# An expert stage with its SBUF divided anew: six buffers instead of three for split weight pieces, 22 weight slabs in turn instead of 26

## The chip, the cores and the metric

The kernel runs on one core of a Trainium2 chip. Its engines are TensorE (PE in the profile; PEld is its weight load), VectorE (DVE), ScalarE (ACT), GpSimd (POOL) and SyncE (SP). Each has a queue of its own that runs strictly in order, and waits for the others through semaphores. The metric is the device time of one execution in microseconds (us); the time of a kernel is the median of several executions.

## What is computed

One block of a model: a token mixer (retention and an mLSTM, 512 tokens and 16 meta tokens, width 1024), then a layer of 16 experts in which each expert chooses its 66 tokens, then a norm. The change lies in the expert layer:

```python
def _rmsnorm(x, g):
    xf = x.astype(jnp.float32)
    y = xf * lax.rsqrt(jnp.mean(xf * xf, axis=-1, keepdims=True) + EPS)
    return (y * g.astype(jnp.float32)).astype(x.dtype)

def _expert_choice_ffn(h, norm_g, w_router, w_gate, w_up, w_down):
    b_, n_, _ = h.shape
    u = _rmsnorm(h, norm_g)
    aff = jax.nn.softmax(jnp.einsum('bnd,de->bne', u, w_router).astype(jnp.float32), axis=-1)
    cap = EC_CAPACITY * n_ // N_EXPERTS
    g, idx = lax.top_k(jnp.swapaxes(aff, 1, 2), cap)
    xs = jax.vmap(lambda ub, ib: ub[ib])(u, idx)
    hid = (jax.nn.silu(jnp.einsum('becd,edf->becf', xs, w_gate))
           * jnp.einsum('becd,edf->becf', xs, w_up))
    y = jnp.einsum('becf,efd->becd', hid, w_down) * g[..., None].astype(h.dtype)
    return jnp.zeros_like(h).at[jnp.arange(b_)[:, None, None], idx].add(y)

def reference(x, meta_tokens, ...):
...
    h = jnp.concatenate([meta, x], axis=1)
    for l in range(DEPTH):
        h = h + _token_mixer(h, mix_norm_g[l], w_in[l], ...)
        h = h + _expert_choice_ffn(h, ffn_norm_g[l], w_router[l], w_gate[l], w_up[l], w_down[l])
    h = _rmsnorm(h, final_norm_g)
    return h[:, N_META:]
```

Here n_ is 528, cap is 66, and an expert's hidden width is 2816. All of it is float32.

## The kernel before

**Stages.** The mixer and the routing take the first 437 us or so. The rest is the expert stage, `experts` (L852 ff.), with its SBUF laid out by `expert_memory` (L733 to L749).

**An expert.** Its weights (34.6 MB) come through SBUF as 48 slabs of 128 x 1408 float32 (704 KB each): eight for the first half of w_gate, eight for the first half of w_up, eight and eight for the second halves, sixteen for w_down. `weights` (L873) takes the next slab space in turn and issues the load on SP's queue (L878; three of them on POOL, L877). The spaces in turn are `ring`, 26 slabs, after a first pass over 29 spaces (`order`, L748); a load must wait until VectorE, the last reader of a space, is done with it.

**Pieces.** The products are made exact to float32 by splitting both operands into a rounded high part and a remainder. `product` (L892) cuts each slab into two or three pieces (768 and 640 columns; 512, 512 and 384 at the first slab of eight; w_down's cuts rotate). For each piece `split` (L885) has ScalarE copy it to h (L888) and VectorE subtract h from the slab into l (L889); then TensorE multiplies the 66 tokens' high part with h (L903), their low part with h (L904), and their high part with l (L905). The buffers for h and for l are a ring of three each, in the space `pieces` (L860 and L861, `right5t` in the profile). A piece can thus be split only when the piece three before it has been multiplied.

**Order within an expert.** In `experts`, for expert e: w_gate's first half, silu on ScalarE (`gate`, L937); w_up's first half, product on VectorE (`up`, L943); two slabs of w_gate's second half, then `hidden(hT, 0)`, which transposes hid on TensorE (L949), copies it on ScalarE (L952) and takes the remainder on VectorE (L953); the rest of w_gate and w_up; three slabs of w_down, then `hidden(hT, 1)` and `gather(e + 1)`, whose eight transposes (L916) are followed by VectorE's gains (L921) and ScalarE's copies (L922); the rest of w_down; `scatter`, in which ScalarE scales the two output halves (L1006) and POOL adds them to the rows in DRAM. The stretch around the transposes of `hidden(hT, 1)` and `gather` is called the boundary below.

**The last expert** goes through w_down twice, for one half of the output columns each (`last_down`). `combine(0)` adds the first half to the rows between: ScalarE scales (L992), TensorE multiplies by a selection (L998, L999), VectorE adds (L1000), ScalarE squares (L1059).

**What sets the order.** The program's text gives the dependences; a scheduler with a simulated clock then orders each engine's instructions, so that buffers added in one place can move instructions in another. The names in the profile: `left25t` is hid, `left26t` to `left29t` are `low`, `left30t` holds the tokens' high and low parts, `left31t` the output rows, `left32t` to `left53t` the slabs of `mid`, `left54t` and `left55t` the two of `early`, `left56t` the transposed hid.

Of the kernel before, what the change touches and what calls it, by code (L numbers as in the profile page):

```python
# [9 lines left out]
F32R = mybir.dt.float32r  # L10
# [28 lines left out]
PIECE = 768  # L39
# [693 lines left out]
def expert_memory(left, ctx):  # L733
    P = 128

    def slabs(stack, n):
        return [left.open(stack, SLAB).tile(P, SLAB) for _ in range(n)]

    brief = ExitStack()
    hid, = slabs(ctx, 1)  # L740
    low = slabs(ctx, 4)
    xs = left.open(ctx, 2 * KT * CAP, F32R)
    y_rows = left.open(ctx, 2 * D).t
    mid = slabs(ctx, 22)
    early = slabs(brief, 2)
    up = mid[::-1]
    ring = up[:12] + low + up[12:]
    order = itertools.chain(ring[:7], [hid], ring[7:16], early, ring[16:], itertools.cycle(ring))  # L748
    return brief, hid, xs, (order, len(ring)), [t[:, :D] for t in mid[7:0:-1]], mid[0], y_rows  # L749


# [100 lines left out]
def experts(tc, a, bcast, left, right, routed, u_rows, h_rows, out):  # L852
    nc = tc.nc
    P = 128
# [3 lines left out]
    with ExitStack() as ctx:  # L858
        ps = ctx.enter_context(tc.tile_pool(name="eps", bufs=1, space=PSUM, reuse_waits="tile"))
        pieces = right.open(ctx, 6 * PIECE, F32R)  # L860
        p_h, p_l = pieces.ring(3, P, PIECE), pieces.ring(3, P, PIECE)  # L861
        x_h, x_l = xs.tile(P, KT, CAP), xs.tile(P, KT, CAP)
        xf = xf.rearrange("p (k c) -> p k c", c=CAP)
        g_exp = moe.tile(P, KT)
# [15 lines left out]

        def bank(tag="wide"):
            return ps.tile([P, 512], F32, name=tag, bufs=6 if tag == "wide" else 2)

        def split(src):
            n = src.shape[1]  # L885
            h = next(p_h)[:, :n]
            l = next(p_l)[:, :n]
            nc.scalar.activation(h, src, AF.Copy)  # L888
            nc.vector.tensor_sub(l, src, h)  # L889
            return h, l  # L890
# [34 lines left out]
        def wide(w, e, half):  # L925
            src = w[e].rearrange("(p k) f -> p k f", k=KT)
            banks = [bank() for _ in range(3)]
            for k in range(KT):
                slab = weights(src[:, k, half * SLAB:(half + 1) * SLAB])
                product(slab, 0, (512, 1024) if k == 0 else (768,),  # L930
                        lambda c: (banks[c], x_h[:, k], x_l[:, k], k == 0, k == KT - 1))
                yield banks

        def gate(banks):
            for c, b in enumerate(banks):
                n = min(512, SLAB - 512 * c)
                nc.scalar.activation(hid[:CAP, 512 * c:512 * c + n], b[:CAP, :n], AF.Silu)  # L937

        def up(banks):
            for c, b in enumerate(banks):  # L940
                n = min(512, SLAB - 512 * c)
                s = slice(512 * c, 512 * c + n)
                nc.vector.tensor_mul(hid[:CAP, s], b[:CAP, :n], hid[:CAP, s])  # L943

        def hidden(hT, half):
            for f0, fn in ((0, 6), (6, 5)):
                b = bank("wide" if half else "narrow")
                for j in range(fn):
                    nc.tensor.transpose(b[:, j * CAP:(j + 1) * CAP], hid[:CAP, f0 + j:SLAB:RH], ident[:CAP, :CAP])  # L949
                v = b[:, :fn * CAP].rearrange("p (k c) -> p k c", c=CAP)  # L950
                s = slice(RH * half + f0, RH * half + f0 + fn)
                nc.scalar.activation(hT[:, 0, s], v, AF.Copy)  # L952
                nc.vector.tensor_sub(hT[:, 1, s], v, hT[:, 0, s])  # L953
# [49 lines left out]
        def scatter(e, banks):  # L1003
            y = next(y_rows)
            for i, b in enumerate(banks):
                nc.scalar.activation(y[:, 512 * i:512 * i + 512], b[:CAP], AF.Copy, scale=val_t[:CAP, e:e + 1])  # L1006
            nc.gpsimd.indirect_dma_start(  # L1007
                out=h_rows, out_offset=bass.IndirectOffsetOnAxis(ap=idx_t[:CAP, e:e + 1], axis=0),
                in_=y, in_offset=None, compute_op=ALU.add)

        def run(steps, n=None):
            out = None
            for out in itertools.islice(steps, n):
                pass
            return out
# [4 lines left out]
        for e in range(E):  # L1020
            g = wide(a["w_gate"], e, 0)
            gate(run(g))
            up(run(wide(a["w_up"], e, 0)))
            g = wide(a["w_gate"], e, 1)
            run(g, 2)
            if hT is None:
                brief.close()
                space = left.open(ctx, 2 * FT * CAP, F32R).t
                hT = space.rearrange("p (a b c) -> p a b c", b=FT, c=CAP)
            hidden(hT, 0)  # L1030
            gate(run(g))
            up(run(wide(a["w_up"], e, 1)))
            if e == E - 1:
                break
            d = down(e, hT)
            run(d, 3)
            hidden(hT, 1)
            gather(e + 1)
            scatter(e, run(d))
# [8 lines left out]
        slabs = itertools.cycle([next(slabs) for _ in range(n_slabs - 5)])  # L1048
# [98 lines left out]
```

## Time and profile before

| | |
|---|---|
| median of 3 runs | 2024.74 us (2024.28 to 2026.84) |
| the profiled execution's own time | 2024.38 us |
| its span in the trace | 2022.7 us |
| busy: PE, PEld, DVE, ACT, POOL | 96%, 74%, 89%, 75%, 17% |
| DMA, the weight queue q1 | 76.1% of 16 engines' span |
| chain that ended last, by engine | PE 73%, DVE 2%, ACT 2%, issue 1% |

Busy shares are averages over the whole span. The chain is followed back from the last instruction, at each step to what released it. A matmul's row gives the time until its modelled end, which overlaps with the next one's start.

### The profile page before, as it was taken

Reading aid. Unit: us, or ns where it says so; the run is one execution under the profiler, and the core shown is the slowest. Engines: PE = TensorE matmul, PEld = TensorE weight load, DVE = VectorE, ACT = ScalarE, POOL = GpSimd, SP = SyncE. Lnnn points to the kernel's source line nnn. Section 1 sums busy time; section 2 is a strip of 40 time slices with the busy share of each in tenths; the row PEclk is TensorE's granted clock in tenths of the full one; section 3 lists DMA queues with packets and bytes.
Section 4 is the critical chain, followed back from the end, with each engine's and each line's share of the span. In section 5 each row is a group of like instructions: output and inputs, shape, how many; then the busy total and the mean of one; then the engine's idle time right before and its main releaser. Section 6 shows DMA issues by size and latency. Waiting matters only on the chain.

```text
span 2022.7 us, 34626 instructions
## 1 busy us (share of the span) xinstructions
PE 1935.0 (96%) x11841; PEld 1494.8 (74%) x11841; DVE 1793.8 (89%) x2612; ACT 1515.4 (75%) x2398; POOL 335.5 (17%) x301
## 2 busy tenths in 40 slices
PE   7888899959999999999999999999999999999997
PEld 7888899847777777777777767676777776767674
DVE  8999988469999999999999898989898989898988
ACT  4455445358888888888888888888888888888886
POOL 4677764400000000000000000000000000000002
PEclk9999999979999999999999999999999999999998
DMA  4222224698999999999999999999999999999971
GB/s 147 81 64 80 75 75 145 252 345 313 359 365 374 354 381 352 383 351 375 360 366 361 360 358 362 356 364 346 366 343 366 347 365 351 365 352 361 345 254 69
DMA packets 136772, 606.25 MB, mean 300 GB/s; under 512 B 19887, under 2 KB 20527, under 8 KB 136595
## 3 DMA queue, kind: packets, MB, share of 16 engines
q1 hardware_dynamic: 125827, 570.55, 76.1%
q10 hardware_dynamic: 6656, 22.29, 3.2%
q0 software_dynamic: 4112, 11.21, 2.4%
q8 instruction: 92, 1.51, 0.3%
q14 instruction: 85, 0.70, 0.1%
HBM read 593.41 MB, written 10.57 MB: 299 GB/s over the span
## 4 chain that ended last, share of the span: by engine, by line
PE 73%; DVE 2%; ACT 2%; issue 1%; POOL 0%; POOLq 0%; DVEq 0%; ACTq 0%
PE wide L903 16%; PE wide L904 15%; PE wide L905 15%; PE narrow L905 8%; PE narrow L903 8%; PE narrow L904 8%; ACT right5t L888 2%; DVE right5t L889 1%; PE wide L949 1%; PE narrow L949 1%; PE wide L916 1%; DVE left25t L943 0%; DVE left56t L953 0%; ACT wide L1059 0%; POOL right3t L1065 0%
## 5 line engine op out<-in xcount | busy, mean ns | idle before, releaser
L904 PE MATMUL wide<-right5t,left30t 128*66 128x256 f32 (+2 forms) x1984 | 639.2, 327 | 0.0
L903 PE MATMUL wide<-right5t,left30t 128*66 128x256 f32 (+2 forms) x1984 | 624.1, 329 | 5.9 <-ACT right5t L888 1.7
L905 PE MATMUL wide<-right5t,left30t 128*66 128x256 f32 (+2 forms) x1984 | 497.3, 328 | 0.1
L903 PEld LDWEIGHTS wide<-right5t,left30t 128*66 128x66 f32 x1984 | 270.8, 137 | 102.7 <-ACT right5t L888 24.5
L905 PEld LDWEIGHTS wide<-right5t,left30t 128*66 128x66 f32 x1984 | 265.9, 137 | 92.2 <-DVE right5t L889 2.8
L903 PE MATMUL narrow<-right5t,left56t 128*66 128x512 f32 x884 | 307.6, 352 | 2.7 <-ACT right5t L888 2.7
L904 PEld LDWEIGHTS wide<-right5t,left30t 128*66 128x66 f32 x1984 | 270.3, 136 | 52.6 <-issue 0.4
L904 PE MATMUL narrow<-right5t,left56t 128*66 128x512 f32 x884 | 302.4, 352 | 0.0
L905 PE MATMUL narrow<-right5t,left56t 128*66 128x512 f32 x884 | 268.8, 354 | 3.6 <-DVE right5t L889 3.2
L909 POOL DMA_INDIRECT right3t<-u_rows,right3t x16 | 15.7, 981 | 939.0 <-PE narrow L905 457.6
L903 PEld LDWEIGHTS narrow<-right5t,left56t 128*66 128x66 f32 x884 | 122.5, 139 | 58.7 <-ACT right5t L888 3.5
L904 PEld LDWEIGHTS narrow<-right5t,left56t 128*66 128x66 f32 x884 | 122.7, 139 | 55.8 <-issue 3.1
L905 PEld LDWEIGHTS narrow<-right5t,left56t 128*66 128x66 f32 x884 | 114.0, 141 | 57.6 <-DVE right5t L889 12.7
L210 PE MATMUL pj<-right1t,left2t 128*128 128x256 f32 (+1 forms) x512 | 149.3, 292 | 0.6 <-DVE left24t L382 0.6
L212 PE MATMUL pj<-right1t,left3t 128*128 128x272 f32 (+1 forms) x512 | 149.5, 292 | 0.1
L211 PE MATMUL pj<-right2t,left2t 128*128 128x272 f32 (+1 forms) x512 | 148.8, 291 | 0.0
L369 POOL TENSOR_TENSOR left3t<-left1t,left2t 128x1024 fp32r<-128x1024 f32 x38 | 98.4, 2590 | 57.5 <-ACT left2t L368 49.1
L210 PEld LDWEIGHTS pj<-right1t,left2t 128*128 128x128 f32 x512 | 99.5, 195 | 0.8 <-DVE left24t L382 0.7
L212 PEld LDWEIGHTS pj<-right1t,left3t 128*128 128x128 f32 x512 | 99.0, 193 | 0.5 <-DVE left3t L369 0.4
L211 PEld LDWEIGHTS pj<-right2t,left2t 128*128 128x128 f32 x512 | 99.2, 194 | 0.1
L1007 POOL DMA_INDIRECT h_rows<-left31t,right3t x15 | 22.4, 1496 | 415.3 <-ACT left31t L1006 415.3
L943 DVE TENSOR_TENSOR left25t<-wide,left25t 66x512 f32<-66x512 f32 (+1 forms) x96 | 58.5, 637 | 19.2 <-PE wide L905 19.2
(405 smaller groups left out, 4294.9 us busy)
## 6 DMA issues: line engine op xcount, KB each, us to landing
left1t<-in_w_in_f ACTq DMA_DIRECT2D x30, 512.0 KB
left29t<-in_w_gate SPq DMA_DIRECT2D x11, 704.0 KB
left41t<-in_w_gate SPq DMA_DIRECT2D x11, 704.0 KB
left38t<-in_w_gate SPq DMA_DIRECT2D x11, 704.0 KB
left37t<-in_w_gate SPq DMA_DIRECT2D x11, 704.0 KB
left52t<-in_w_up SPq DMA_DIRECT2D x11, 704.0 KB
left51t<-in_w_up SPq DMA_DIRECT2D x11, 704.0 KB
left53t<-in_w_gate SPq DMA_DIRECT2D x10, 704.0 KB
```

The costliest lines, as they stand in the source:

```text
L210: nc.tensor.matmul(ps[:, :ln], wh, x_h[:, k, l0:l0 + ln], start=(k == 0), stop=False)
L211: nc.tensor.matmul(ps[:, :ln], wh, x_l[:, k, l0:l0 + ln], start=False, stop=False)
L212: nc.tensor.matmul(ps[:, :ln], wl, x_h[:, k, l0:l0 + ln], start=False, stop=(k == KT - 1))
L369: eng.tensor_sub(l, t, h)
L888: nc.scalar.activation(h, src, AF.Copy)
L889: nc.vector.tensor_sub(l, src, h)
L903: nc.tensor.matmul(o, xh, h[:, w], start=start, stop=False)
L904: nc.tensor.matmul(o, xl, h[:, w], start=False, stop=False)
L905: nc.tensor.matmul(o, xh, l[:, w], start=False, stop=last)
L943: nc.vector.tensor_mul(hid[:CAP, s], b[:CAP, :n], hid[:CAP, s])
L949: nc.tensor.transpose(b[:, j * CAP:(j + 1) * CAP], hid[:CAP, f0 + j:SLAB:RH], ident[:CAP, :CAP])
L1007: nc.gpsimd.indirect_dma_start(out=h_rows, out_offset=bass.IndirectOffsetOnAxis(ap=idx_t[:CAP, e:e + 1], axis=0), in_=y, in_offset=None, c ...
```

## The change

`expert_memory` makes 18 slabs of `mid` instead of 22 and six of `early` instead of two. The six are used first, once each; the spaces in turn are 22 instead of 26. The first pass has 29 spaces as before. In expert 0, when `brief` (the early slabs' space) is closed, `more_pieces` opens a second piece space there, `left57t`, with three more buffers for h and three more for l; from then on the ring of each is six: three on the right, three on the left. `left56t` stays the transposed hid; the early slabs are now `left50t` to `left55t`. From L885 on, line numbers are 6 higher than before, from L1040 on 7.

```diff
@@ -741,11 +741,11 @@
     low = slabs(ctx, 4)
     xs = left.open(ctx, 2 * KT * CAP, F32R)
     y_rows = left.open(ctx, 2 * D).t
-    mid = slabs(ctx, 22)
-    early = slabs(brief, 2)
+    mid = slabs(ctx, 18)
+    early = slabs(brief, 6)
     up = mid[::-1]
-    ring = up[:12] + low + up[12:]
-    order = itertools.chain(ring[:7], [hid], ring[7:16], early, ring[16:], itertools.cycle(ring))
+    ring = up[:8] + low + up[8:]
+    order = itertools.chain(early[::-1], ring[:1], [hid], ring[1:], itertools.cycle(ring))
     return brief, hid, xs, (order, len(ring)), [t[:, :D] for t in mid[7:0:-1]], mid[0], y_rows
 
 
@@ -858,7 +858,8 @@
     with ExitStack() as ctx:
         ps = ctx.enter_context(tc.tile_pool(name="eps", bufs=1, space=PSUM, reuse_waits="tile"))
         pieces = right.open(ctx, 6 * PIECE, F32R)
-        p_h, p_l = pieces.ring(3, P, PIECE), pieces.ring(3, P, PIECE)
+        halves = [[pieces.tile(P, PIECE) for _ in range(3)] for _ in range(2)]
+        p_h, p_l = map(itertools.cycle, halves)
         x_h, x_l = xs.tile(P, KT, CAP), xs.tile(P, KT, CAP)
         xf = xf.rearrange("p (k c) -> p k c", c=CAP)
         g_exp = moe.tile(P, KT)
@@ -880,6 +881,11 @@
 
         def bank(tag="wide"):
             return ps.tile([P, 512], F32, name=tag, bufs=6 if tag == "wide" else 2)
+
+        def more_pieces():
+            nonlocal p_h, p_l
+            a = left.open(ctx, 6 * PIECE, F32R)
+            p_h, p_l = (itertools.cycle(v + [a.tile(P, PIECE) for _ in range(3)]) for v in halves)
 
         def split(src):
             n = src.shape[1]
@@ -1027,6 +1033,7 @@
                 brief.close()
                 space = left.open(ctx, 2 * FT * CAP, F32R).t
                 hT = space.rearrange("p (a b c) -> p a b c", b=FT, c=CAP)
+                more_pieces()
             hidden(hT, 0)
             gate(run(g))
             up(run(wide(a["w_up"], e, 1)))
```

VectorE in expert 12, from the up-products of the second half (before L943, then L949) over the boundary (gains L921, then L927; remainders of hid L953, then L959); the pieces' remainders are L889, then L895. Before:

```order
L943 TENSOR_TENSOR left25t<-wide,left25t 66x512
L943 TENSOR_TENSOR left25t<-wide,left25t 66x384
L889 TENSOR_TENSOR right5t<-left46t,right5t 128x512
L889 TENSOR_TENSOR right5t<-left46t,right5t 128x384
L889 TENSOR_TENSOR right5t<-left45t,right5t 128x640
L921 TENSOR_TENSOR right3t<-wide,right3t 128x264
L953 TENSOR_TENSOR left56t<-wide,left56t 128x396
L921 TENSOR_TENSOR right3t<-wide,right3t 128x264
L889 TENSOR_TENSOR right5t<-left45t,right5t 128x768
L953 TENSOR_TENSOR left56t<-wide,left56t 128x330
L889 TENSOR_TENSOR right5t<-left44t,right5t 128x768
```

and with the change:

```order
L949 TENSOR_TENSOR left25t<-wide,left25t 66x512
L949 TENSOR_TENSOR left25t<-wide,left25t 66x384
L895 TENSOR_TENSOR right5t<-left42t,right5t 128x512
L895 TENSOR_TENSOR right5t<-left42t,right5t 128x384
L895 TENSOR_TENSOR right5t<-left26t,right5t 128x640
L895 TENSOR_TENSOR left57t<-left26t,left57t 128x768
L927 TENSOR_TENSOR right3t<-wide,right3t 128x264
L959 TENSOR_TENSOR left56t<-wide,left56t 128x396
L927 TENSOR_TENSOR right3t<-wide,right3t 128x264
L959 TENSOR_TENSOR left56t<-wide,left56t 128x330
L895 TENSOR_TENSOR left57t<-left27t,left57t 128x768
```

The fifth remainder of w_down (768 columns) now stands ahead of the gains; before, it stood behind these and the first remainder of hid.

ScalarE in the last expert, at the silus of the first half (before L937, then L943); the pieces' copies are L888, then L894. Before:

```order
L888 ACTIVATE right5t<-left35t 128x640
L888 ACTIVATE right5t<-left34t 128x512 x2
L937 ACTIVATE left25t<-wide 66x512
L888 ACTIVATE right5t<-left34t 128x384
L937 ACTIVATE left25t<-wide 66x512
L937 ACTIVATE left25t<-wide 66x384
L888 ACTIVATE right5t<-left33t 128x768
```

and with the change:

```order
L894 ACTIVATE right5t<-left37t 128x640
L894 ACTIVATE right5t<-left36t 128x512
L894 ACTIVATE left57t<-left36t 128x512
L894 ACTIVATE left57t<-left36t 128x384
L943 ACTIVATE left25t<-wide 66x512 x2
L943 ACTIVATE left25t<-wide 66x384
L894 ACTIVATE left57t<-left35t 128x768
```

The copy of the third piece of w_up's first slab (384 columns) stood between the first silu and the second; it now stands ahead of the three.

ScalarE in expert 0, at the fourth to seventh slab of w_gate's first half, with the change:

```order
L894 ACTIVATE right5t<-left52t 128x768
L894 ACTIVATE right5t<-left52t 128x640
L894 ACTIVATE right5t<-left51t 128x768
L894 ACTIVATE left57t<-left41t 128x640
L894 ACTIVATE right5t<-left51t 128x640
L894 ACTIVATE left57t<-left40t 128x768
L894 ACTIVATE left57t<-left40t 128x640
L894 ACTIVATE right5t<-left50t 128x768
L894 ACTIVATE right5t<-left50t 128x640
L894 ACTIVATE right5t<-left49t 128x768
L894 ACTIVATE right5t<-left49t 128x640
```

Three copies into the new buffers, of the last slab of the first pass's `up[8]` and its neighbour (`left41t`, `left40t`), stand among those of `left51t` and `left50t`; in the program's text they belong to w_gate's second half, fourteen slabs later. Before, the copies of expert 0 followed the order of the slabs. VectorE's remainders move in the same way.

## Rows read from the trace of the kernel before

**Rows 1.** The page, busy time, share of the span and instructions of each engine.
```profile
PE 1935.0 (96%) x11841; PEld 1494.8 (74%) x11841; DVE 1793.8 (89%) x2612; ACT 1515.4 (75%) x2398; POOL 335.5 (17%) x301
```

**Rows 2.** The chain of waits: start us, us on the chain, what.
```profile
503.63 0.23 PE narrow L903
...
506.66 0.88 PE wide L916 x8
...
1083.77 0.88 PE wide L916 x8
...
1378.70 0.88 PE wide L916 x8
...
1873.84 0.88 PE wide L916 x8
```

**Rows 3.** Busy by stretch: length, PE, PEld, DVE, ACT, POOL, PEclk, DMA share, GB/s.
```profile
506.50:602.70 96.20, 95.95 (x573) 71.43 (x572) 89.02 (x121) 81.30 (x123) 4.56 (x4) 1.00 0.98 366
1083.60:1181.90 98.30, 97.15 (x572) 71.04 (x572) 88.30 (x121) 81.31 (x124) 4.99 (x4) 1.00 0.97 358
1379.00:1478.00 99.00, 98.16 (x572) 72.01 (x572) 88.47 (x120) 81.48 (x123) 4.53 (x4) 0.98 0.97 356
```

**Rows 4.** Weight queue: its waits (500 to 1900; us, times, longest), one slab's issue, first use.
```profile
SPq L878 <- DVE right5t L889: 1117.5, 685, 3.9
...
1339.18 0.33 SPq L878 DMA_DIRECT2D left52t<-in_w_down  x1
...
1393.43 1.15 ACT L888 ACTIVATE right5t<-left52t 128x512 fp32r<-128x512 f32 x2
```

**Rows 5.** Waits of the stretch 1181.9 to 1280.2: us in total, times, longest.
```profile
PEld wide L903 <- ACT right5t L888: 2.2, 4, 0.6
...
PEld narrow L905 <- DVE right5t L889: 1.2, 3, 0.6
...
PEld wide L949 <- DVE left25t L943: 0.6, 1, 0.6
```

**Rows 6.** Timeline behind the scatter: start, us, what, [idle before, releaser].
```profile
1212.86 1.24 ACT L1006 ACTIVATE left31t<-narrow,right3t 66x512 f32<-66x512 f32 x2
...
1214.19 0.57 PE L905 MATMUL wide<-right5t,left30t 128*66 128x512 f32 x2
1214.89 0.45 PE L903 MATMUL wide<-right5t,left30t 128*66 128x512 f32 x1
```

**Rows 7.** Timeline at the silus of the first half.
```profile
1229.69 1.47 ACT L888 ACTIVATE right5t<-left53t 128x768 fp32r<-128x768 f32 x2
...
1230.11 0.34 PE L905 MATMUL wide<-right5t,left30t 128*66 128x384 f32 x1
1230.59 0.45 PE L903 MATMUL wide<-right5t,left30t 128*66 128x512 f32 x1
```

**Rows 8.** Timeline at the first up-product.
```profile
1245.03 0.85 ACT L888 ACTIVATE right5t<-left45t 128x768 fp32r<-128x768 f32 x1 [0.49 <-DVE right5t L889]
...
1245.92 0.45 PE L903 MATMUL wide<-right5t,left30t 128*66 128x512 f32 x1 [0.17 <-ACT right5t L888]
```

**Rows 9.** Timeline at the boundary.
```profile
1278.82 1.55 PE L949 MATMUL wide<-right3t,left25t 66*128 66x66 f32 x11 [0.27 <-DVE left25t L943]
...
1279.75 0.81 DVE L889 TENSOR_TENSOR right5t<-left33t,right5t 128x640 fp32r<-128x640 f32 x1
```

**Rows 10.** Busy by stretch, just behind the boundary of expert 10.
```profile
1379.66:1383.10 3.44, 3.44 (x13) 2.32 (x12) 3.44 (x7) 2.60 (x6) 2.75 (x3) 0.51 0.82 264
```

**Rows 11.** Timeline of the last expert, combine(0).
```profile
1990.87 0.60 ACT L1059 ACTIVATE wide<-left35t 128x512 f32<-128x512 f32 x1 [1.96 <-DVE left35t L1000]
...
1993.34 1.13 ACT L888 ACTIVATE right5t<-left28t 128x512 fp32r<-128x512 f32 x2
...
1994.00 0.62 PE L903 MATMUL narrow<-right5t,left56t 128*66 128x512 f32 x1 [2.26 <-ACT right5t L888]
...
1995.55 0.69 PE L905 MATMUL narrow<-right5t,left56t 128*66 128x512 f32 x1 [0.50 <-DVE right5t L889]
...
2000.14 0.45 PE L905 MATMUL narrow<-right5t,left56t 128*66 128x512 f32 x1 [0.69 <-DVE right5t L889]
```

## The prediction

> **What bounds the kernel now.** I read the page first: TensorE is busy for 96% of the span [rows 1], so what can be won is idle TensorE time and time at a low clock. Second, the chain of waits, for the period of an expert. The eight transposes of the next expert's tokens start at 506.66, 1083.77, 1378.70 and 1873.84 us [rows 2]; six experts lie between the first two, three between the next two, five between the last two. Counted from one such start to the next, experts 1 to 6 take (1083.77 - 506.66)/6 = 96.19 us each, experts 7 to 9 take 98.31, experts 10 to 14 take 99.03. The work is the same in each; 2.1 and 2.8 us per expert are waiting or a low clock. Third, busy time by stretch: in an early expert VectorE works 89.02 of 96.20 us and the DMA engines are busy 0.98 of the time, in a late one 88.30 of 98.30 and 0.97 [rows 3]. VectorE has 7 to 10 us to spare per expert, so it is not the bound over an expert, only after bursts. Fourth, the weight queue: from 500 to 1900 us it waited 685 times for VectorE to free a slab, and no row has an engine waiting for a weight transfer; one slab issued at 1339.18 was first read at 1393.43, 54 us later [rows 4].
>
> Fifth, what TensorE waits for in a late expert. The waits of the stretch 1181.9 to 1280.2 give its weight loads four waits for ScalarE's copy of a piece (h), three for VectorE's remainder (l), and one for VectorE's up-product before the hidden transposes [rows 5]. I call them by place:
> - **B**, after the scatter's scaling. ScalarE scales both output halves from 1212.86 (1.24 us) and only then copies the next piece. A 512-column matmul takes 0.23 us of the chain [rows 2], a 384-column one 0.17 by its columns; so TensorE would be done with the pair begun at 1214.19 (512 and 384 columns) at about 1214.60, and goes on at 1214.89: 0.29 us [rows 6].
> - **C** and **E**, after each half's silu. ScalarE comes to the next piece only at 1229.69, behind its silus; TensorE could go on 0.17 after 1230.11 and does at 1230.59: 0.30 us [rows 7]. E is the same 33 us later.
> - **D**, the first up-product. The copy of the next piece waits 0.49 us for VectorE to free a buffer, starts at 1245.03 and holds TensorE until 1245.92: 0.33 us [rows 8].
> - **A**, the three waits for l just after the boundary: the burst of seven VectorE operations there (three up-products, two gains, two remainders of hid) puts l late, 1.2 us at the weight loads [rows 5]; I put two thirds of it, 0.8, on the matmuls, as a weight load runs ahead of its matmul.
> - **F**, the boundary itself: the transposes of hid wait for the third up-product, 0.27 us on the row of the transposes [rows 9], 0.6 at their weight load [rows 5]; I take 0.45.
> Together 2.5 us, which with the jitter of the rest is the 2.1 us above the early experts. In experts 10 to 14 the clock is granted at half (0.51, 1.2 instead of 2.4 GHz) for 3.44 us just behind F [rows 10]; that would cost 3.44 x 0.49 = 1.7, but wait A hides behind it, so that the period grows by 0.72 only.
>
> **The change part by part.**
> Four slabs fewer in turn. A slab is then asked for 22 slabs ahead of its use instead of 26. A slab lasts 96.2/48 = 2.0 us, so the 54 us between issue and use shrink by 4 x 2.0 = 8 to about 46 [rows 4]. The queue's wait for VectorE stays the last one: cost 0. If this cover were gone, each missing slab would cost its 2 us; I price that at nothing since 46 us remain, and a loss would need transfers several times later than now.
>
> Early slabs in expert 0. Six instead of two slabs are used once; they come first, so their space is free when the piece buffers are opened in it. The first pass is 29 slabs either way. Cost 0.
>
> Three pieces pulled forward in expert 0. The order shows pieces of left41t and left40t split between those of left51t and left50t, some fourteen slabs before they are needed. They put 3 pieces on VectorE (0.81 for 640 columns [rows 9], so 2.5 us) and on ScalarE ahead of pieces TensorE needs at once, while only three buffers serve these. TensorE loses 0 (if the lead of two pieces of 0.7 covers it, and the gain of three finished pieces later is used) to 2.5 us. I take +1.2, near the middle, since two pieces' lead is 1.4 us and 2.5 - 1.4 = 1.1.
>
> Six buffers in experts 1 to 3: the order keeps copies and remainders some six pieces ahead. Today's early experts lose little, so 0.
>
> Experts 4 to 6: the order of the late experts begins here at expert 5, not at 7, expert 4 changing over. They leave 96.2 for the new late period, worked out next: 96.7, +0.5 each, +1.5.
>
> Experts 7 to 9: what goes? C and E: the third piece of the next slab was copied between the silus, now all three are copied ahead of them; ScalarE then does the second and third silu as soon as their bank is complete, some 0.3 us earlier, and copies the next piece in time: 0.30 each goes. D goes (0.33), as the copy no longer waits for a buffer. A: VectorE now does one more piece ahead of the burst, 0.8 us, so about 0.6 of the 0.8 goes. B stays: ScalarE's two scalings begin as soon as the last matmul of the output ends, and the copy of the fourth piece follows them in the new order as in the old. F stays: TensorE's order there is unchanged, and VectorE's up-products wait for TensorE's own last bank. So 0.60 + 0.33 + 0.6 = 1.5 to 1.6 of 98.31 goes, to 96.7: 3 x -1.6 = -4.8. Bounds: none goes (0), or the period becomes that of the best rows, 96.19 (-6.4).
>
> The Trainium skill, Perfetto Trace Analysis, section Optimization Strategy, says that the same gap repeating on the engine that should be saturated can mean there is not enough SBUF for the next tile (the number of buffers). By it all six gaps would go; the rows agree for D alone without question, as there a buffer is waited for, and at B and F they name work, not space. I go by the rows.
>
> Experts 10 to 14: to the same 96.7 without the low clock, 5 x (96.7 - 99.03) = -11.6. Bounds 0 and 5 x (96.19 - 99.03) = -14.2.
>
> Low clock at other boundaries. As F stays, some new boundaries may meet it. The price is the 1.7 of [rows 10] less the 0.2 of wait A that it hides, 1.5. At present the stretches of experts 1 and 7 stand at 1.00, that of expert 10 at 0.98 [rows 3], and the equal periods say the same of their neighbours. Of the eleven from expert 4 on I take two: +3.0, bounds 0 and 16.5. The Trainium skill, TensorE: Matmul & The Clock Gate, section on the second failure mode (psum-queue depth-cycling), has short idles between groups make the clock swing; by it fewer idles would mean no low clock, and the sum would be 3.0 lower. The row puts the low clock behind F, which stays, so I keep the two.
>
> Last expert. ScalarE does the four squares of the first output half in a row from 1990.87, the next pieces only at 1993.34; TensorE stands 2.26 us and then runs six matmuls at half clock (0.62 instead of 0.40 each by the rows), with two waits for l of 0.50 and 0.69 in and behind them [rows 11]. In the new order the squares lie between pieces, and three more pieces are ready, 3 x 0.69 = 2.1 us of TensorE's work (three 512-column matmuls each). So 2.1 goes, of the half clock 6 x 0.2 = 1.2, of the two waits for l three quarters, 0.9: -4.2, bounds 0 and -4.7.
>
> Sum: 1.2 + 1.5 - 4.8 - 11.6 + 3.0 - 4.2 = -14.9. The profiled execution took 2024.38 us, 1.7 more than its span and 0.4 below the median of the runs (2024.74); so **2009.5 us**.
>
> **The rivals.**
> 1. *All gaps go.* The finer lead also takes B and F away, the period is everywhere that of the early experts now: 3 x -2.12 + 5 x -2.84 + 1.2 - 4.2 = -23.6, **2000.8 us**. For it: VectorE has spare time to build a lead of six. Against it: at B and F the waiting work depends on TensorE's own last matmul.
> 2. *Slower: the late order everywhere, and the low clock at each boundary.* ScalarE's and VectorE's queues run in a fixed order; if in practice their lead at the boundary is cut to two pieces whatever the buffers (ScalarE must wait there for the hid transposes), A and the rest stay, and the late order with its low clock starts at expert 4 instead of 7 or 10: experts 4 to 6 go from 96.19 to 99.03 (+8.5), 7 to 9 to 99.03 (+2.2), expert 0 +1.2: **2036.3 us**. It decides if the lead after the boundary isn't rebuilt within the next slab and F meets the low clock at nearly every boundary. For it: the order that this change gives is the late one from expert 5 on. Against: VectorE does one more piece before its burst.
> 3. *No effect.* Buffers aren't what the waits hang on; late experts keep 98.31 and 99.03, experts 5 and 6 join them (+4.2), expert 0 +1.2, the last expert still gains 4.2: **2025.6 us**. For it: of the waits only D names a buffer. Against: C, E and A turn on one or two pieces more in hand.
> 4. *The ring is too short* and transfers show: against it stand 46 us. Only a small chance, in with the second.
>
> **How the numbers follow.** Chances: forecast 0.60, rival 1 0.13, rival 2 (with 4) 0.13, rival 3 0.14. A measurement of this kernel tells 0.2% from no change, 4 us, so same is 2020 to 2029. Forecast and rival 1 are faster: 0.73; rival 3 is mostly within: 0.14; rival 2 is slower: 0.13. The forecast's own range, with two or three of its bounds at once, is 2003 to 2017. For 8 in 10, the range goes down to rival 1 and a little below, 1999, and up to where most of rival 3 lies, 2025.
>
> **What would show it.** Right: periods near 96.2 up to expert 3 and near 96.7 after; the waits of TensorE's weight loads for ScalarE's copies once per late expert (B) instead of four times; no stand of 2 us in the last expert; the granted clock at 1.00 over most late boundaries; the weight queue still waiting for VectorE, never an engine for a slab. Wrong: half clock at most boundaries, waits A, C and E at their old length, or an expert 0 longer by over 3 us.

## The result, and the profile after

The changed kernel takes 2004.2 us (median of 4 runs, 2004.15 to 2006.03), the kernel before 2025.8 in the same comparison: ratio 0.9891, 95% interval 0.988 to 0.9903, so about 1.1% faster. The forecast was 2009.5, inside a range of 1999 to 2025. The profiled execution's span is 2002.4 us, 20.3 less than before; all differences below are differences of spans.

The page of the changed kernel, busy time by engine:

```profile
PE 1924.2 (96%) x11841; PEld 1498.6 (75%) x11841; DVE 1745.8 (87%) x2612; ACT 1443.0 (72%) x2398; POOL 476.0 (24%) x301
```

Against [rows 1], TensorE's share is as high as it was. Its work is the same; its busy time fell by 10.8 us and its idle time by 9.5. About 4 us of the fall in busy time is less time at half clock, estimated from the mean granted clock (0.983 over 2002.4 us, before 0.981 over 2022.7); the rows do not split the rest.

The chain of waits, the start of the eight transposes of expert 5, 7, 8, 10 and 15 (start, us on the chain, what):

```profile
889.77 0.89 PE wide L922 x8
...
1082.48 0.88 PE wide L922 x8
...
1180.42 0.88 PE wide L922 x8
...
1374.71 0.89 PE wide L922 x8
...
1859.58 0.88 PE wide L922 x8
```

Experts 5 and 6 take (1082.48 - 889.77)/2 = 96.36 us each; expert 7 takes 97.94; experts 10 to 14 take 96.97 on average, where they took 99.03 [rows 2]. Busy time by stretch, for experts 1, 7 and 10 (us; PE, PEld, DVE, ACT, POOL busy; PEclk, DMA share, GB/s):

```profile
510.10:605.50 95.40, 95.40 (x573) 71.66 (x572) 87.09 (x121) 78.91 (x123) 5.09 (x4) 1.00 0.98 370
...
1082.30:1180.30 98.00, 97.73 (x573) 72.34 (x573) 85.50 (x121) 76.33 (x123) 9.72 (x4) 0.98 0.97 360
...
1374.50:1470.90 96.40, 96.14 (x573) 71.38 (x572) 85.08 (x121) 76.01 (x123) 21.62 (x4) 1.00 0.97 365
```

Three things stand out against [rows 3]. Expert 1 has no idle TensorE time at all: 95.40 of 95.40 us. Late experts have two periods now, 96.4 and 97.9, and the longer one goes with a mean clock of 0.98. And GpSimd, busy 4.5 to 5 us per expert before, is busy 21.62 us in some experts; the last section returns to that. What TensorE waits for in expert 10 (us in total, times, longest):

```profile
PEld wide L955 <- DVE left25t L949: 0.6, 1, 0.6
PEld wide L909 <- ACT right5t L894: 0.4, 1, 0.4
PEld narrow L955 <- DVE left25t L949: 0.3, 1, 0.3
PEld narrow L911 <- DVE left57t L895: 0.3, 1, 0.3
PE wide L955 <- DVE left25t L949: 0.3, 1, 0.3
PEld wide L909 <- ACT left57t L894: 0.2, 1, 0.2
```

Against [rows 5]: the waits for ScalarE's copies fell from 2.2 to 0.6 us, those for VectorE's remainders from 1.2 to 0.3, and the wait of the hidden transposes for the third up-product (F) is the same 0.6. These are waits of weight loads, and only part of each reaches the matmuls: F is 0.6 at the weight load and 0.3 at the transposes themselves. The timeline behind the scatter, at place B [rows 6]:

```profile
1404.52 1.26 ACT L1012 ACTIVATE left31t<-narrow,right3t 66x512 f32<-66x512 f32 x2 [1.55 <-PE narrow L911]
...
1406.06 0.57 PE L911 MATMUL wide<-left57t,left30t 128*66 128x512 f32 x2
1406.56 0.45 PE L909 MATMUL wide<-right5t,left30t 128*66 128x512 f32 x1
```

The pair begun at 1406.06 ends near 1406.47, so the gap is 0.1 us; it was 0.29. ScalarE now stands idle for 1.55 us before its scalings, which wait for TensorE's last matmul of w_down; the next copy stands behind them in its queue.

The half clock, behind the boundary of expert 7 and of expert 8 (same columns as the stretches above):

```profile
1082.50:1085.90 3.40, 3.40 (x18) 2.44 (x18) 3.40 (x8) 3.38 (x7) 2.16 (x2) 0.65 0.91 260
...
1180.50:1183.90 3.40, 3.40 (x25) 2.64 (x24) 3.40 (x8) 3.40 (x7) 2.22 (x2) 1.00 0.93 266
```

By their periods in the chain, experts 7, 9, 11 and 14 have it (97.9), the other seven from 4 to 14 do not. It costs 97.94 - 96.36 = 1.6 us each time. The weight queue from 500 to 1900 us still waits for VectorE, in 366 and 314 waits [rows 4]. One wait of ScalarE in expert 10, 0.6 us, is put down to a weight transfer; before there was none.

```profile
SPq L879 <- DVE left57t L895: 572.4, 366, 6.0
SPq L879 <- DVE right5t L895: 519.5, 314, 5.0
```

In the last expert the squares lie between pieces, and the stand of 2.26 us [rows 11] is gone; two short waits for VectorE remain later, of which this is the first:

```profile
1976.64 0.60 ACT L1066 ACTIVATE wide<-left33t 128x512 f32<-128x512 f32 x1 [0.33 <-DVE left33t L1006]
...
1977.35 0.63 ACT L894 ACTIVATE right5t<-left45t 128x512 fp32r<-128x512 f32 x1
...
1984.50 0.45 PE L911 MATMUL narrow<-right5t,left56t 128*66 128x512 f32 x1 [0.70 <-DVE right5t L895]
```

Where the 20.3 us came from, by differences of these starts:

| stretch | forecast | measured |
|---|---|---|
| up to the first transposes (435.51 to 436.75) | 0 | +1.2 |
| experts 1 to 3, 96.19 to 95.41 each | 0 | -2.3 |
| experts 0 and 4 to 6 | +2.7 | -0.2 |
| experts 7 to 14 (790.1 to 777.1), half clock included | -13.4 | -13.0 |
| last expert, from its transposes to the end of the span (148.9 to 142.8) | -4.2 | -6.0 |

### The profile page after: what moved, and what is told of

Read it like the earlier page. It is cut to its first block, busy times and chain, and to the rows that moved or that the text cites. A ratio compares the mean times of both kernels' runs of the same rounds, so it can differ in the third digit from the quotient of the medians.

```text
span 2002.4 us, 34495 instructions
## 1 busy us (share of the span) xinstructions
PE 1924.2 (96%) x11841; PEld 1498.6 (75%) x11841; DVE 1745.8 (87%) x2612; ACT 1443.0 (72%) x2398; POOL 476.0 (24%) x301
## 4 chain that ended last, share of the span: by engine, by line
PE 82%; DVE 10%; issue 2%; ACT 2%; POOL 1%; DMA 1%; POOLq 0%; SPq 0%; DVEq 0%; ACTq 0%
PE wide L909 16%; PE wide L910 16%; PE wide L911 16%; PE narrow L911 8%; PE narrow L909 8%; PE narrow L910 8%; DVE left19t L479 2%; PE wide L955 1%; PE narrow L955 1%; DVE left6t L426 1%; PE pj L210 1%; PE pj L212 1%; PE pj L211 1%; DVE left25t L949 1%; PE wide L922 1%
## 5 line engine op out<-in xcount | busy, mean ns | idle before, releaser
L910 PE MATMUL wide<-right5t,left30t 128*66 128x512 f32 (+2 forms) x996 | 322.9, 329 | 0.0
L909 PE MATMUL wide<-right5t,left30t 128*66 128x256 f32 (+2 forms) x996 | 316.9, 329 | 0.9 <-ACT left30t L928 0.5
L910 PE MATMUL wide<-left57t,left30t 128*66 128x256 f32 (+2 forms) x988 | 314.8, 326 | 0.0
L909 PE MATMUL wide<-left57t,left30t 128*66 128x256 f32 (+2 forms) x988 | 314.4, 326 | 0.0
L911 PE MATMUL wide<-right5t,left30t 128*66 128x512 f32 (+2 forms) x996 | 254.1, 329 | 0.3 <-DVE right5t L895 0.3
L911 PE MATMUL wide<-left57t,left30t 128*66 128x256 f32 (+2 forms) x988 | 245.3, 326 | 0.0
L929 POOL TENSOR_TENSOR left30t<-right3t,left30t 128x264 fp32r<-128x264 f32 x30 | 171.8, 5743 | 71.2 <-ACT left30t L928 70.4
L909 PEld LDWEIGHTS wide<-left57t,left30t 128*66 128x66 f32 x988 | 134.8, 136 | 48.4 <-ACT left57t L894 1.7
L909 PEld LDWEIGHTS wide<-right5t,left30t 128*66 128x66 f32 x996 | 136.1, 137 | 42.1 <-ACT right5t L894 4.9
L911 PEld LDWEIGHTS wide<-right5t,left30t 128*66 128x66 f32 x996 | 134.4, 138 | 43.7 <-DVE right5t L895 0.7
L911 PEld LDWEIGHTS wide<-left57t,left30t 128*66 128x66 f32 x988 | 132.2, 136 | 38.4
L910 PEld LDWEIGHTS wide<-left57t,left30t 128*66 128x66 f32 x988 | 134.4, 136 | 33.6
L910 PE MATMUL narrow<-right5t,left56t 128*66 128x512 f32 x443 | 153.5, 352 | 0.0
L910 PEld LDWEIGHTS wide<-right5t,left30t 128*66 128x66 f32 x996 | 135.8, 136 | 23.0 <-issue 0.4
L909 PE MATMUL narrow<-right5t,left56t 128*66 128x512 f32 x443 | 152.3, 351 | 0.0
L909 PE MATMUL narrow<-left57t,left56t 128*66 128x512 f32 (+1 forms) x441 | 151.5, 349 | 0.0
L910 PE MATMUL narrow<-left57t,left56t 128*66 128x512 f32 (+1 forms) x441 | 147.4, 348 | 0.0
L911 PE MATMUL narrow<-right5t,left56t 128*66 128x512 f32 (+1 forms) x442 | 134.2, 354 | 0.7 <-DVE right5t L895 0.7
```

The costliest lines, as they stand in the source:

```text
L909: nc.tensor.matmul(o, xh, h[:, w], start=start, stop=False)
L910: nc.tensor.matmul(o, xl, h[:, w], start=False, stop=False)
L911: nc.tensor.matmul(o, xh, l[:, w], start=False, stop=last)
L929: (nc.gpsimd if e else nc.vector).tensor_sub(x_l[:, sl], v, x_h[:, sl])
```

## The experiments

The theory: TensorE loses time where an in-order queue puts an operation that TensorE itself has to release ahead of pieces that TensorE needs next; buffers let ScalarE and VectorE do those pieces beforehand. Its rivals: the slabs' places did it; one of the two buffer kinds did it; the new order of instructions did it, whatever the buffers. This last rival is tested by moving single operations; the change's own order was not run with three buffers, since a piece cannot be copied ahead of its buffer.

### The slabs alone

```diff
                 hT = space.rearrange("p (a b c) -> p a b c", b=FT, c=CAP)
-                more_pieces()
             hidden(hT, 0)
```

> The new division of the slabs (18 + 6, 22 in turn) without the new piece buffers: the ring stays at three. Theory (the lead of the pieces decides): as before the change, 2025 us within 3, periods 96.2, 98.3 and 99.0 in the three groups of experts. Rival (the slabs' places or their order decide): 2004 us.

Measured: 2027.6 us, ratio to before 1.0004 (0.9994 to 1.0014). The new division by itself neither costs nor gains: four slabs fewer in turn are covered, and the gain comes only with the buffers. The order still changes a little: the late order begins at expert 6, with periods of 98.4 and, with the half clock, 99.1.

### One kind of buffer

```diff
-            p_h, p_l = (itertools.cycle(v + [a.tile(P, PIECE) for _ in range(3)]) for v in halves)
+            p_h = itertools.cycle(halves[0] + [a.tile(P, PIECE) for _ in range(3)])
```

> Six buffers for h (ScalarE's copies), three for l. Theory 1 (both leads are needed, each takes its own waits away): C, D and E go, A and F stay: late experts near 97.2, 2013 us within 4. Theory 2 (VectorE is the late one, so only l counts): 2022 us or more. Theory 3 (only h counts): 2004 us.

Measured: 2026.5 us, ratio 0.9995 (0.9984 to 1.0007). Busy time by stretch for experts 1, 5 and 8, then TensorE's waits in expert 8:

```profile
507.10:604.70 97.60, 96.85 (x573) 71.16 (x572) 88.10 (x121) 77.85 (x123) 4.60 (x4) 1.00 0.97 361
898.80:997.80 99.00, 98.25 (x573) 72.14 (x572) 88.54 (x121) 77.75 (x123) 4.29 (x4) 0.98 0.96 356
1194.40:1291.90 97.50, 96.67 (x573) 71.25 (x572) 88.05 (x121) 76.19 (x123) 5.33 (x4) 1.00 0.97 362
```

```profile
PEld narrow L911 <- DVE right5t L895: 1.7, 4, 0.6
PEld wide L955 <- DVE left25t L949: 0.6, 1, 0.6
...
PEld wide L909 <- ACT right5t L894: 0.4, 1, 0.4
...
PEld wide L909 <- ACT left57t L894: 0.2, 1, 0.2
```

The total is 13 us above what theory 1 gave, but the late expert is near to it, 97.5 instead of 98.3 (expected 97.2): the waits for copies went from 2.2 to 0.6 us, those for remainders grew from 1.2 to 1.7 [rows 5]. What the expectation missed is the early experts, 1.4 to 2.8 us longer than before. In expert 5 both transposes of hid now wait for the up-product, and four weight loads for remainders:

```profile
PEld wide L911 <- DVE right5t L895: 1.4, 4, 0.5
PEld wide L955 <- DVE left25t L949: 0.6, 1, 0.6
PEld narrow L955 <- DVE left25t L949: 0.6, 1, 0.6
```

Experts 4 to 6 have a stretch at half clock as well (the 0.98 above), experts 1 to 3 have none. So the sum came to nothing. That the new order, with more copies in hand and no more remainders, left VectorE behind there fits these waits, but was not tested by itself.

```diff
-            p_h, p_l = (itertools.cycle(v + [a.tile(P, PIECE) for _ in range(3)]) for v in halves)
+            p_l = itertools.cycle(halves[1] + [a.tile(P, PIECE) for _ in range(3)])
```

> Six buffers for l (VectorE's remainders), three for h. Theory 1 (both are needed): ScalarE can still copy only three pieces ahead, so C, D and E stay and only part of A goes: 2020 us within 4. Theory 2 (only l counts): 2004 us. Theory 3 (only h counts): 2025 us.

Measured: 2028.1 us, ratio 1.0004 (0.9995 to 1.0014), where theory 1 gave 2020. Experts 1 and 8:

```profile
508.80:604.70 95.90, 95.90 (x573) 71.41 (x571) 88.16 (x121) 81.17 (x124) 4.24 (x4) 1.00 0.98 367
1187.00:1285.40 98.40, 97.25 (x573) 71.16 (x572) 87.93 (x121) 81.44 (x124) 4.99 (x4) 1.00 0.96 358
```

Early experts gain 0.3 us, late ones nothing (98.4 here, 99.1 where the half clock is): VectorE can't subtract what ScalarE has not copied. So neither kind is "the one that counts"; the shorter of the two leads does, and the gains don't add up from the two halves (0 + 0 against 20).

### Four instead of six

```diff
-            p_h, p_l = (itertools.cycle(v + [a.tile(P, PIECE) for _ in range(3)]) for v in halves)
+            p_h, p_l = (itertools.cycle(v + [a.tile(P, PIECE) for _ in range(1)]) for v in halves)
```

> Four buffers for each instead of six, all else as in the change. If one more piece in hand is what the late experts lacked: late periods at 96.3 to 96.6 as with six, early ones between 95.4 and 96.2, 2006 us within 3. If the gain grows with each buffer: a third of it, 2018 us.

Measured: 2005.2 us (2003.54 to 2005.7), ratio 0.9886 (0.9869 to 0.9902). Experts 1 and 7:

```profile
508.50:604.20 95.70, 95.70 (x573) 71.52 (x572) 87.86 (x122) 80.19 (x124) 7.18 (x4) 1.00 0.98 367
1083.20:1179.50 96.30, 96.03 (x573) 71.33 (x572) 86.29 (x121) 80.03 (x123) 9.71 (x4) 1.00 0.97 366
```

One more piece in hand is what the late experts lacked; 96.3 with four as with six. The other two buffers are worth 0.3 us in an early expert, and 2.7 in the last one (145.7 us from its transposes to the end of the span, against 143.0); in the total they can't be told from none.

### The ring shorter still

```diff
-    mid = slabs(ctx, 18)
-    early = slabs(brief, 6)
+    mid = slabs(ctx, 14)
+    early = slabs(brief, 10)
     up = mid[::-1]
-    ring = up[:8] + low + up[8:]
+    ring = up[:4] + low + up[4:]
```

> Six buffers, but 18 slabs in turn and ten early ones. Theory (the weight transfers have some 46 us in hand, 38 with four slabs fewer): as the change, 2004 us within 2. Rival (the slabs in turn are near their limit): each expert longer by 1 us or more, 2020 us.

Measured: 2015.7 us (2014.21 to 2016.86), ratio 0.994 (0.9924 to 0.9957), so a miss of the total. Expert 0 and expert 7:

```profile
434.90:512.20 77.30, 73.21 (x427) 55.54 (x428) 65.43 (x88) 61.01 (x89) 0.99 (x1) 0.94 0.70 252
1086.70:1183.00 96.30, 96.03 (x572) 71.31 (x572) 85.02 (x121) 76.06 (x123) 21.61 (x4) 1.00 0.96 366
```

Expert 7 takes the same 96.3 with 18 slabs in turn, so the theory's reason holds in the experts between the first and the last. The loss lies at the two ends, and this kernel does not compute the block: its output is wrong. With ten early slabs the space of hid (`left25t`) becomes the twelfth in turn instead of the eighth. In expert 0 a slab of w_up is loaded into it on top of the silus, before the up-product reads them (that space takes a slab only once, so the later experts' times are not touched by this):

```profile
456.22 0.59 ACT L943 ACTIVATE left25t<-wide 66x512 f32<-66x512 f32 x1
458.84 0.33 SPq L879 DMA_DIRECT2D left25t<-in_w_up  x1
474.03 0.69 DVE L949 TENSOR_TENSOR left25t<-wide,left25t 66x512 f32<-66x512 f32 x1 [0.22 <-PE wide L911]
```

TensorE is idle 4.1 us in expert 0 (1.2 in the change), of which 1.4 us is a wait for the copy of that slab; so the time of expert 0 says nothing of the ring's length. The last expert is 7 us longer, and the cause of that is open. Of the ring's length this run shows the steady part only.

### F, and the half clock

```diff
             d = down(e, hT)
-            run(d, 3)
-            hidden(hT, 1)
+            run(d, 2)
+            behind = newest[0].ins
+            run(d, 1)
+            with tc.issue_after(behind):
+                hidden(hT, 1)
```

Here `newest[0]` is the last matmul issued (L911 in the changed kernel); the last expert's w_down has the same edit. In the rows of this run and of all that follow, line numbers are one higher than in the kernel that was edited.

> The change, and in each expert the transposes of the second half of hid (and with them the next tokens') are issued on TensorE only behind the second slab of w_down, so that VectorE's up-products are done when TensorE comes to them. Theory (F is the start of the half-clock stretches, and the late order is only a transposition too early): periods of 95.4 in all experts 1 to 14, clock 1.00 in all of them, the last expert 0.9 shorter: 1987 us within 3. Rival (the half clock comes from something else at the boundary, the transposes themselves): the gap F goes, the half clock stays at some boundaries, 1993 us or more.

Measured: 2006.7 us (2006.33 to 2008.62), ratio to before 0.9896 (0.988 to 0.9913): no gain over the change, 20 us above the 1987 expected. Expert 7, and TensorE ahead of the boundary at its end:

```profile
1087.20:1184.40 97.20, 96.33 (x572) 71.38 (x572) 85.91 (x121) 76.48 (x123) 4.34 (x4) 1.00 0.97 363
```

```profile
1179.87 0.45 PE L912 MATMUL narrow<-right5t,left56t 128*66 128x512 f32 x1 [0.87 <-DVE right5t L896]
```

Half of the theory is borne out: without a wait before the transposes the clock stays at 1.00, and the periods of experts 5 to 14 all lie between 97.17 and 97.21, none longer for a half clock. The traces of all thirteen kernels here, those below included, say the same. Where the transposes of hid at the end of an expert wait 0.15 to 0.34 us, a half clock follows at 44 of 91 boundaries; where they wait 0.1 us or less, at none of 104. So in these runs the half clock needs the wait, and the wait alone does not bring it: what decides between the 44 and the other 47 is open. The other half fell: TensorE now waits about as long (0.87 us by the row) for the remainder of w_down's second piece, which stands in VectorE's queue behind the last two up-products. F was the place where VectorE's burst showed, not its cause.

> The same edit on the kernel before: three buffers, 26 slabs in turn. Theory (buffers decide the waits A, C, D and E; the edit takes F and the half clock away): 9 x 0.45 and 5 x 0.7 go, 2017 us within 3, late periods near 97.8. Rival (the place of the transposes made the late order bad, and the buffers only cured it): every expert like the early ones, 96.2, 2004 us.

Measured, the same edit with three buffers: 2026.4 us, ratio 0.9993 (0.9984 to 1.0003). TensorE's waits in expert 8 there:

```profile
PEld wide L904 <- ACT right5t L889: 2.2, 4, 0.6
...
PE narrow L906 <- DVE right5t L890: 0.9, 1, 0.9
```

The four waits for copies are those of [rows 5] unchanged; the late periods are 98.4 with no half clock, and a wait of 0.9 us for a remainder stands where F was. Neither sum held (2017 and 2004): the buffers do decide the waits for copies, as the theory has it, but the edit again only moved the boundary's wait.

### VectorE's burst behind the pieces

```diff
-            up(run(wide(a["w_up"], e, 1)))
+            banks = run(wide(a["w_up"], e, 1))
             if e == E - 1:
+                up(banks)
                 break
             d = down(e, hT)
-            run(d, 3)
+            run(d, 1)
+            with tc.issue_after(newest[0].ins):
+                up(banks)
+            run(d, 2)
             hidden(hT, 1)
```

Here `newest[0]` is VectorE's newest remainder (L895 in the changed kernel).

> The change, and VectorE's three up-products of the second half are issued behind its remainders of w_down's first slab (three pieces), the transposes of hid following them. If F and the wait for l that took its place both come from VectorE's burst standing between pieces that TensorE needs at once: neither is left, no stretch at half clock, late periods 95.4 to 95.7, 1990 us within 3. Rival (the burst is late wherever it stands, as VectorE can start it only when TensorE's up bank is complete): a wait of 0.5 to 1 us at the boundary again, 2003 us or more.

Measured: 2006.4 us (2005.37 to 2007.42), ratio 0.9902 (0.9885 to 0.9918). The total is at the rival's number (2003 or more), but not for the rival's reason: no matmul waits at the boundary of expert 7 any more. The new order has a wait elsewhere. ScalarE and TensorE in expert 7, at the silus of the first half:

```profile
1130.03 0.60 ACT L944 ACTIVATE left25t<-wide 66x512 f32<-66x512 f32 x1 [4.30 <-PE wide L912]
1130.53 0.62 ACT L895 ACTIVATE right5t<-left42t 128x512 fp32r<-128x512 f32 x1
...
1131.19 0.45 PE L910 MATMUL wide<-right5t,left30t 128*66 128x512 f32 x1 [0.56 <-ACT right5t L895]
```

ScalarE, with buffers free, stands 4.30 us in front of a silu that waits for TensorE, and the copy that TensorE needs next lies behind it. The period is 97.2 with the clock at 1.00.

> The same edit on the kernel before (three buffers). If the buffers decide: VectorE cannot have three remainders ready and three more being used, so the boundary still waits for l, C, D and E stay, 2024 us within 4. Rival (the order at the boundary decides, whatever the buffers): late periods near 96.2, 2004 us.

Measured, three buffers: 2019.1 us (2016.74 to 2020.34), ratio 0.9962 (0.9948 to 0.9976), 5 us below the expectation. Its waits in expert 8:

```profile
PEld wide L904 <- ACT right5t L889: 2.2, 4, 0.6
PEld wide L950 <- DVE left25t L944: 0.6, 1, 0.6
```

With three buffers the edit does take A away in the late experts, and the half clock (period 97.2, down from 98.3 and 99.0), against the expectation; of F, 0.6 us is left at the weight load and 0.1 at the transposes. The waits for copies, 2.2 us [rows 5], stay to the digit, as expected. So in the late experts the boundary hangs on the order, the copies on the buffers. In the early ones the same edit brings a wait of 0.34 us ahead of the transposes that was not there, and two of them, 3 and 5, then have a half clock and take 97.9.

### The silus behind the copies too

```diff
-            gate(run(g))
-            up(run(wide(a["w_up"], e, 0)))
+            banks = run(g)
+            u = wide(a["w_up"], e, 0)
+            run(u, 1)
+            with tc.issue_after(newest[1].ins):
+                gate(banks)
+            up(run(u))
```

This comes on top of the edit above, in both halves; `newest[1]` is ScalarE's newest copy (L894 in the changed kernel). "The run before last" in the expectation is the one with six buffers and the up-products behind.

> The run before last (six buffers, up-products behind the first slab of w_down), and ScalarE's silus are issued behind its copies of the next slab's three pieces, both halves. Theory (with six buffers each wait that is left is a place where an operation that TensorE itself must release stands in a queue ahead of pieces that are already needed; with those moved nothing waits): late periods 95.5, no half clock, 1990 us within 3. Rival (there is a floor near 96.3 for late experts, set by the engines' busy time): 2000 us or more.

Measured: 1993.3 us (1990.92 to 1993.68), ratio to before 0.9831 (0.9818 to 0.9844): faster than both kernels, and just beyond the 1990 within 3 that was expected. Experts 2 and 7:

```profile
604.80:700.20 95.40, 95.40 (x573) 71.67 (x572) 87.06 (x121) 78.92 (x123) 5.05 (x4) 1.00 0.98 369
1080.80:1176.60 95.80, 95.80 (x573) 71.50 (x572) 85.22 (x120) 76.27 (x123) 4.26 (x4) 1.00 0.98 369
```

By these rows no idle TensorE time is left in a late expert, and no half clock. The floor at 96.3 was not one. A late expert still takes 0.4 us more than an early one; two of its weight loads wait for copies, 0.4 and 0.2 us.

> The same two edits on the kernel before, three buffers. Theory (order and buffers are both needed: with three buffers the fourth piece can't be copied ahead of the silus): some waits at the silus stay, late periods 96.2 to 97, 2012 us within 4. Rival (the order alone does it): as with six buffers, 1992 us.

Measured, three buffers: 2029.9 us (2026.69 to 2033.93), ratio 1.0013 (1.0004 to 1.0022): 18 us above what the theory gave, and slower than with the up-products moved alone (2019.1). TensorE's waits in expert 8:

```profile
PEld wide L904 <- ACT right5t L889: 3.0, 4, 0.9
PE wide L904 <- ACT right5t L889: 1.1, 3, 0.5
```

The order that gives six buffers 1993 us gives three buffers nothing: the waits for copies grow from 2.2 to 3.0 us. Three pieces ahead of the silus fill a ring of three, so the fourth copy can only come late. Order and buffers are both needed for the 1993 us.

## Why the prediction was right, step by step

The direction and the main cause were right: with more pieces in hand, most waits of the late experts went. The size was 5.3 us short, and the table above shows where: experts 1 to 3, expert 0 with 4 to 6, and the last one gained more than forecast.

- **Fewer slabs in turn, early slabs: 0.** Right; the slabs alone gave 1.0004.
- **Expert 0: +1.2.** Too high. The first transposes come 1.2 us later (436.75 against 435.51), but that is ahead of the expert stage. Nothing ties this to the change: over the other traces this start lies between 435.7 and 438.2 with the old division of the slabs and between 434.6 and 438.1 with the new one. Within expert 0 the three pieces pulled forward cost little: its stretch of 73.3 us has 1.2 us of idle TensorE time, against 0.8 in the 71.0 before (the boundary lies about 2.2 us of matmuls further on in the new order, which expert 4 gives back).
- **Experts 1 to 3: 0.** Wrong by 2.3 us. "Today's early experts lose little" overlooked the 0.8 us that separate 96.19 from a full TensorE; with six buffers they run at 95.40, all busy.
- **Experts 4 to 6: +1.5.** Wrong in the level: the late period is 96.36, not 96.7, which is 0.17 above the early one of before.
- **Experts 7 to 14: -16.4, less 3.0 for the half clock.** The sum is right, -13.0 against -13.4, by two misses that cancel, which is luck. A, C, D and E went as the steps said. B was said to stay and went from 0.29 to 0.1: before, ScalarE came to its scalings straight from a copy, without idling [rows 6], so they began when that copy was done and not when TensorE's output was. With six buffers the copies are done earlier, and the scalings wait for TensorE alone. F stayed, as said. Against that, the half clock came at four boundaries of eleven, not two; its price, 1.5, was right (1.6).
- **The six gaps and the half clock, by rule and by row.** The Trainium skill, Perfetto Trace Analysis, Optimization Strategy, says that a gap that repeats can mean too little room for the next tile; read so, all six would go with more buffers. Four and most of a fifth went, and F did not; F went in the runs with six buffers and another order. So that reading is wrong in F and the one by rows in B, and the time lies nearer to the first (2000.8) than to the second (2009.5). The Trainium skill, TensorE: Matmul & The Clock Gate, second failure mode, has short idles between groups of matmuls make the clock swing. Here fewer idles did not end the half clock (four of eleven boundaries), and ending the one at F did (none of the boundaries of experts 5 to 14 in the runs without it at six buffers). The traces side with the place of the idle, ahead of a stretch of transposes.
- **The last expert: -4.2.** Too small: -6.0, beyond the bound of -4.7, which counted the waits around the first combine alone. There the three waits of [rows 11] went from 3.5 to 1.4 us (forecast -3.0, measured -2.0), and the half clock went. The step put the boundary into this expert at nothing. Before, a half clock stood behind it, and in the change there is none (the first row is of the kernel before):

```profile
1874.60:1878.10 3.50, 3.50 (x15) 2.23 (x13) 3.50 (x7) 2.49 (x6) 1.53 (x2) 0.51 0.75 224
...
1859.40:1862.90 3.50, 3.50 (x27) 2.79 (x27) 3.50 (x7) 3.39 (x8) 1.08 (x1) 1.00 0.95 277
```

- **Rivals.** The first, that all gaps go (2000.8), lies nearer to the measured 2004.2 than the forecast does. It was nearly right on the period, 96.36 against its 96.19, and wrong on F and the half clock. The second (the late order everywhere with its half clock) was right that the late order starts at expert 5, and wrong on its price, since the order differs by the one piece that decides. The third, that buffers aren't what the waits hang on, fell with the slabs alone and the runs of one kind against both. The fourth, a ring too short, fell with the slabs alone.

## What to carry to other kernels

Where two engines prepare pieces for a third, the shorter of their leads decides: doubling the buffers of one may give nothing, and one more piece for both may give nearly all. Buffers pay in full only if each in-order queue has its pieces ahead of the operation that must wait; after adding buffers, look for an idle stretch of a preparing engine in front of an operation that the bound engine releases (here 4.30 us), and move that operation behind the pieces. A wait that is cured by moving the waiting instruction may only show up elsewhere, as twice here; move the work that makes it late.

## What was not expected of the hardware

GpSimd's subtraction of 128 x 264 elements behind the boundary takes 1.09 us in the kernel before (expert 10), and in the changed kernel:

```profile
1376.94 17.99 POOL L929 TENSOR_TENSOR left30t<-right3t,left30t 128x264 fp32r<-128x264 f32 x1
```

It starts 0.3 us before VectorE begins a run of subtractions from SBUF to SBUF (1377.25). It ends 18 us later, at 1394.9, just after VectorE's first pause in that run (0.32 us, up to 1394.64). With the second one GpSimd is busy 21.62 us in that expert. In the version at 1993 us (expert 8) it starts 0.6 us before VectorE's run, and both take 1.79 us together, while three subtractions of VectorE's take 2.31 us instead of 1.75. The Trainium skill, GPSIMD Engine Reference, section Key points, states that GpSimd shares its SBUF interfaces with VectorE and that VectorE's instructions with two SBUF inputs contend with it. The rows agree, and they show that in the changed kernel it was GpSimd that was held back, and in the faster version VectorE; what decides which is not shown. The result is needed by the next expert's first product at about 1404.5 us, so nothing waited for it in this kernel.
